# Filter products as two stacked high/low matmuls, sine layers in three pieces, and the sums of squares woven into the first modulation

## The chip, the core and the metric

The kernel runs on one core of one Trainium2 chip. The time is that of one execution on the device, in microseconds (us); lower is better. Engines: TensorE (PE, its weight loads PEld), VectorE (DVE), ScalarE (ACT), GpSimd (POOL) and SyncE (SP), which issues most of the DMAs.

## The reference, cut to what matters

Two layers of a trunk run over 512 latent tokens and 256 context tokens, 1024 channels wide. Each layer has a modulated norm, one input projection into three head groups (Hyena, neighbourhood attention, latent attention), an output projection and an MLP. The change touches three things at the start of the first layer. The modulation:

```python
def _modulation(cond, w_mod, b_mod):
    m = jax.nn.silu(cond) @ w_mod + b_mod
    return jnp.split(m[:, None, :], 6, axis=-1)
```

the norm, which needs the mean square of every token and the first two of the six modulation blocks (shift and scale), and the Hyena filters, which depend on no token at all:

```python
    hdn = jnp.sin(freq[0] * (z @ w1 + b1))
    hdn = jnp.sin(freq[1] * (hdn @ w2 + b2))
    h = (hdn @ w3 + b3).reshape(L, HY_ORDER, 2, HY_DIM)
    ...
    h = h * decay[:, None, None, :]
    return h / (jnp.sum(jnp.abs(h), axis=(0, 2), keepdims=True) + EPS)
```

z has 17 rows, the hidden layers 64 channels, and the last product gives 1024 columns. The filters are made for both layers with the latent length (512) and for the first layer with the context length (256); their spectra are stored in DRAM and read later by the convolution.

## The kernel before, in words

Activations stand transposed: channels on partitions, tokens (NT = 768) along the row. Large products are made in three passes from a high part (rounded to the type fp32r) and a low part (the rest): high by high, high by low, low by high (`gemm`, L262). `split` (L135) makes such a pair with one ScalarE copy and one VectorE subtraction; `wblock` (L253) does so for a block of weights, with three buffers for each of the raw, high and low tiles.

**The order.** The code is a Python program that is unrolled. Generators are woven by hand: `weave` (L791) steps each generator by its rate, and a fill generator by its own. A scheduler then orders each engine's instructions from that program, taking the earliest one that it takes to be ready; on the chip each engine runs its list in order. SP issues the DMAs in its own list, and a load into a buffer still in use holds up everything behind it.

**The start, L1141 to L1193.** `filter_hidden` (L323) loads z, w1, w2 and constants and makes both sine layers of both trunk layers together (64 channels each, 128 partitions). `sin_layer` (L306) takes 768 columns at once: a ScalarE scale and bias from PSUM (L311), five VectorE instructions that bring the argument into range (L313, L314, twice L317, L319), and a ScalarE sine (L321). The second layer's result goes into `h2`, one tile of 65 rows for each trunk layer, row 64 holding ones for the bias. SP then issues the eight blocks of x (L1153), the last filter weights w3 (65 rows), the decay and the first transform matrix, the eight blocks of the modulation's second part (`wm1`, gains), a small matrix, and the eight blocks of its first part (`wm0`, shifts). The 16 modulation blocks (512 KB each) share 13 buffers. `sumsq` (L207) squares a block of x on ScalarE (L213) and adds it on VectorE (L214); the eight blocks are worked between the two sine layers.

`norm_rstd` (L216) sums the squares over channels with TensorE (L221), takes the reciprocal root on VectorE (L122 to L126), and, on its second call, turns it into a row for all partitions (L232, L233). `modulation` (L145) takes two weight blocks a step with TensorE (L150), yields four times, then turns the result (L155, L158) and writes `mods` (L162).

**The filters' fill.** `spectra` (L1166) goes through six filters. For each token tile of a filter `filter_unit` (L340) makes one step: a product of `h2` and w3 (L350, 128x512, plain fp32), a multiplication by the decay (L353), an absolute value (L356, L360) added up (L361), and a sum and a difference (L362 on VectorE, L363 on GpSimd). Its spectrum follows in two or three steps, by turns with the next filter's: the sums (L370), then eight products for each tile of frequencies (L387) with VectorE additions (L391, L395) and a store from GpSimd's queue (L396). There are 20 steps with a product and 16 of spectra. One step runs ahead of the modulations, five beside them (L1184 to L1186); the rest fill the first input products (`mla_in` L633 at half a step for each k, `na_v` L458 at 0.4), and what is left is run after them.

**The norm, L236.** For each of eight channel blocks and both streams: a VectorE multiplication (L241), a ScalarE scale and shift (L242), and the split into high and low (L136, L137). The first input products (L273) need its first block and the first split weights.

## Time and profile before

| | us |
|---|---|
| Runs of the kernel before (three) | 1832.9, 1833.13, 1833.24 |
| Their median | 1833.13 |
| The profiled execution, own time | 1833.48 |
| Its span, first to last instruction | 1831.7 |

The profile is one execution. A line of it gives the source line, engine, operation, output and input by the program's names, shapes and count. PE records: a plain fp32 product leaves two records, a product of fp32r operands one. "Idle before" and the arrow say how long the engine stood still and what ended that. Windows give busy time of each engine with the number of instructions, the granted TensorE clock (1.00 is 2.4 GHz, 0.50 is 1.2 GHz), the share of DMA time and the rate. Matmul ends are modelled, so prices are read from the rhythm of starts where that can be done.

### The profile page before, as it was taken

How to read it: one execution, taken by the hardware profiler on the slowest of the kernel's cores; microseconds unless marked ns; L12 is line 12 of the kernel's file. 1: busy time of each engine (PE TensorE's matmuls, PEld its weight loads, DVE VectorE, ACT ScalarE, POOL GpSimd, SP SyncE). 2: the span in 40 equal slices, each digit the busy share in tenths (PEclk: the TensorE clock that was granted, in tenths of full speed). 3: DMA queues.
4: the chain of work that ended last, by engine and by line, in shares of the span. 5: the costliest groups of instructions: out<-in, count | busy, mean ns of one | idle time of the engine just before them, and what ended most of it. 6: DMA issues, size and time to landing. Idle time of an engine off the chain costs nothing. (4 is left out here: it accounts for less than half of the span.)

```text
span 1831.7 us, 27057 instructions
## 1 busy us (share of the span) xinstructions
PE 1752.5 (96%) x10794; PEld 1499.4 (82%) x10794; DVE 1233.4 (67%) x2247; ACT 754.7 (41%) x1262; POOL 135.8 (7%) x177
## 2 busy tenths in 40 slices
PE   5999977889999999999999999999999999999999
PEld 2788976756788888888888888888777799999997
DVE  5867777787768877767665447787877665555554
ACT  3624326566734412213212224745666653333331
POOL 1134222200000000000000000231200000000000
PEclk8999989989999999999999999999999999999999
DMA  9225423263153333333332222362041022333232
GB/s 344 72 86 167 148 70 108 82 214 113 53 198 115 138 120 134 117 137 115 130 124 60 67 68 95 114 226 81 24 167 41 31 93 94 97 99 93 93 93 81
DMA packets 73389, 206.11 MB, mean 113 GB/s; under 512 B 12556, under 2 KB 24605, under 8 KB 71856
## 3 DMA queue, kind: packets, MB, share of 16 engines
q1 hardware_dynamic: 71664, 199.15, 32.3%
q0 software_dynamic: 1600, 5.24, 0.8%
q8 instruction: 85, 1.39, 0.3%
q14 instruction: 40, 0.33, 0.1%
HBM read 182.35 MB, written 21.23 MB: 111 GB/s over the span
## 5 line engine op out<-in xcount | busy, mean ns | idle before, releaser
L273 PE MATMUL mm<-t,wh 128*128 128x512 f32 (+1 forms) x2496 | 492.5, 317 | 1.9 <-DVE t L1037 1.3
L136 ACT ACTIVATE wh<-wr 128x1024 fp32r<-128x1024 f32 (+2 forms) x176 | 185.2, 1054 | 599.4 <-PE mm L273 541.4
L273 PEld LDWEIGHTS mm<-t,wh 128*128 128x128 f32 x2496 | 371.4, 189 | 37.9 <-issue 1.9
L273 PE MATMUL mm<-t,wl 128*128 128x512 f32 (+1 forms) x1248 | 296.9, 316 | 0.0
L137 DVE TENSOR_TENSOR wl<-wr,wh 128x1024 fp32r<-128x1024 f32 (+2 forms) x176 | 214.1, 1217 | 30.5 <-ACT wh L136 27.1
L273 PE MATMUL mm<-al,wh 128*128 128x512 f32 (+1 forms) x768 | 233.6, 359 | 0.0
L273 PE MATMUL mm<-ah,wl 128*128 128x512 f32 (+1 forms) x768 | 232.2, 356 | 0.0
L1037 DVE SCALAR_TENSOR_TENSOR t<-mm,mods,t 128x512 f32<-128x512 f32 x216 | 136.3, 659 | 140.6 <-PE mm L273 132.7
L273 PE MATMUL mm<-ah,wh 128*128 128x512 f32 (+1 forms) x768 | 230.9, 354 | 0.0
L273 PEld LDWEIGHTS mm<-t,wl 128*128 128x128 f32 x1248 | 193.6, 189 | 16.2 <-DVE wl L137 0.2
L273 PEld LDWEIGHTS mm<-ah,wl 128*128 128x128 f32 x768 | 127.6, 188 | 22.5
L273 PEld LDWEIGHTS mm<-ah,wh 128*128 128x128 f32 x768 | 126.7, 188 | 23.6
L273 PEld LDWEIGHTS mm<-al,wh 128*128 128x128 f32 x768 | 126.3, 188 | 20.1
L191 DVE SCALAR_TENSOR_TENSOR wmp<-wm,t 128x1024 f32<-128x1024 f32 x64 | 78.3, 1224 | 68.3 <-DMA wm<-in_w_modr_dram 68.3
L425 DVE TENSOR_REDUCE mmx<-mm 128x1 f32<-128x768 f32 (+1 forms) x80 | 67.5, 846 | 24.9 <-PE mm L133 24.2
L136 ACT ACTIVATE ah<-relu 128x768 fp32r<-128x768 f32 (+1 forms) x64 | 47.3, 739 | 87.2 <-DVE relu L1100 87.1
L430 ACT ACTIVATE msb<-mm,mmx,qrs 128x768 f32<-128x768 f32 (+1 forms) x80 | 72.2, 904 | 24.8 <-DVE mmx L427 21.1
L1090 DVE TENSOR_SCALAR bb<-mm,cols 128x2 f32<-128x2 f32 x64 | 14.0, 219 | 97.6 <-PE mm L273 97.4
L191 DVE SCALAR_TENSOR_TENSOR wm<-wm,t 128x1024 f32<-128x1024 f32 x64 | 78.1, 1220 | 0.2
L1001 ACT ACTIVATE mpt<-mm 128x768 f32<-128x768 f32 (+1 forms) x80 | 57.6, 725 | 49.9 <-PE mm L1000 49.8
L137 DVE TENSOR_TENSOR al<-relu,ah 128x768 fp32r<-128x768 f32 (+1 forms) x64 | 52.6, 823 | 36.2 <-ACT ah L136 36.1
L1346 PE MATMUL mm<-t,wh 128*128 128x512 f32 x320 | 76.2, 352 | 0.0
(304 smaller groups left out, 2922.0 us busy)
## 6 DMA issues: line engine op xcount, KB each, us to landing
wr<-in_w_ff_dram SPq DMA_DIRECT2D x128, 512.0 KB, 3.6
wm<-in_w_modr_dram SPq DMA_DIRECT2D x64, 512.0 KB, 4.5
wm<-in_w_mod_dram SPq DMA_DIRECT2D x32, 512.0 KB, 8.4
wr<-in_w_in_t_dram SPq DMA_DIRECT2D x18, 512.0 KB, 4.0
qk<-qk_spill SPq DMA_DIRECT2D x9, 576.0 KB, 5.5
qk_spill<-upk SPq DMA_DIRECT2D x12, 384.0 KB, 2.9
kx<-kk POOLq DMA_DIRECT2D x16, 256.0 KB, 2.5
wr<-in_w_in_qk_dram SPq DMA_DIRECT2D x8, 512.0 KB, 4.6
```

Source lines behind the costliest of these rows:

```text
L136: act.activation(hi, src, AF.Copy)
L137: dve.tensor_sub(lo, src, r32(hi))
L191: dve.scalar_tensor_tensor(w if s else junk, w, 1.0, cr[:, s], ALU.mult, ALU.mult, accum_out=mods[:, l, v, k, s:s + 1])
L273: pe.matmul(out_[:, po:po + b - a], wk[wx], mk[mx][:, a:b], start=(k == 0 and i == 0), stop=(k == nk - 1 and i == 2))
L425: dve.tensor_reduce(mx, src, AX.X, ALU.max, negate=True)
L430: act.activation(sb[:, h, :n], src[:, h, :n], AF.Exp, bias=mx[:, h:h + 1], scale=1.0 if scale is None else scale[:, h:h + 1], accum_out=sm ...
L1001: act.activation(pt[:, 0:nkt, qt * 128:(qt + 1) * 128], tt[:, :nkt * 128].rearrange("p (c q) -> p c q", q=128), AF.Copy)
L1037: dve.scalar_tensor_tensor(xT[:, m, a:b], t[:, a:b], mods[:, l, v, m, s:s + 1], xT[:, m, a:b], ALU.mult, ALU.add)
L1090: dve.tensor_scalar(bb, t[:, 768:770], cols[:, l, C_BF1 + f:C_BF1 + f + 1], None, ALU.add)
L1346: pe.matmul(t[:, a:b], ws[wx], half[mx][:, k % 4, a:b], start=(k == ks[0] and i == 0), stop=(k == 7 and i == 2))
```

## The change

- `sin_layer` works on one piece of 256 columns, with three buffers; `filter_hidden` runs three pieces through both layers, the second layer of a piece behind the first layer of the next.
- The last filter product is made from fp32r operands. For each trunk layer there are two tiles of 128 rows for the hidden layer (the high part with the low part stacked under it, or above it for the second trunk layer; and the high part again with rows of ones) and two for w3 (the high part twice; the low part with the bias, also split). Two products of 512 columns replace one.
- `filter_weights` loads w3 raw (64 rows, and the bias row apart) and splits it: three ScalarE copies, two VectorE subtractions, a clear on GpSimd. For the first trunk layer it stands at the start, for the second in the fill.
- SP issues w3, decay and the first transform matrix ahead of x. The modulation blocks share 10 buffers instead of 13.
- The squares are no longer worked between the sine layers but woven with the first modulation (rate 0.6) and the fill (0.5), after two fill steps; then come the sums over channels, and the second modulation with the fill at 0.8.

```diff
--- before.py
+++ after.py
@@ -303,12 +303,10 @@
         sp.dma_start(t, A[name] if src is None else src)
         return t
 
-    def sin_layer(p, outs, zs, hyc, j):
-
-        fb, arg, k = p([128, 1], tag="fb", bufs=2), p([128, NT], tag="arg"), p([128, NT], tag="argk")
-        dve.tensor_mul(fb, hyc[:, j:j + 1], hyc[:, 2 + j:3 + j])
-        for z, a, b in zs:
-            act.activation(arg[:, a:b], z, AF.Identity, bias=fb, scale=hyc[:, j:j + 1])
+    def sin_layer(p, z, fb, hyc, j, n):
+
+        arg, k = p([128, n], tag="arg", bufs=3), p([128, n], tag="argk", bufs=3)
+        act.activation(arg, z, AF.Identity, bias=fb, scale=hyc[:, j:j + 1])
         magic = 12582912.0
         dve.tensor_scalar(k, arg, 1.0 / (2 * math.pi), magic, ALU.mult, ALU.add)
         dve.tensor_scalar(k, k, magic, None, ALU.subtract)
@@ -317,25 +315,56 @@
             dve.scalar_tensor_tensor(arg, k, -c, arg, ALU.mult, ALU.add)
         lim = 3.1415925
         dve.tensor_scalar(arg, arg, -lim, lim, ALU.max, ALU.min)
-        for o, i in outs:
-            act.activation(o, arg[i], AF.Sin)
+        act.activation(arg, arg, AF.Sin)
+        return arg
+
+    def filter_halves(l):
+        return slice(64 * l, 64 * l + 64), slice(64 - 64 * l, 128 - 64 * l), 64 - 64 * l
 
     def filter_hidden(p, h2):
 
         z, w1, w2 = load(p, "hy_z", [17, NT]), load(p, "hy_w1", [17, 128]), load(p, "hy_w2", [128, 128])
-        hyc = load(p, "hy_c", [128, 4])
-        h1 = p([128, NT])
-        for h in h2:
-            pool.memset(h[64:65, :], 1.0)
+        hyc, fb = load(p, "hy_c", [128, 4]), p([128, 2])
+        for l, (_, b) in enumerate(h2):
+            _, other, r = filter_halves(l)
+            pool.memset(r32(b[other]), 0.0)
+            for r_ in (r, r + 32):
+                pool.memset(r32(b[r_:r_ + 1]), 1.0)
         yield
-        for j, (w, src) in enumerate(((w1, z), (w2, h1))):
-            ts = []
-            for a, b in BOTH:
-                ts.append((b_tile()[:, 0:b - a], a, b))
-                pe.matmul(ts[-1][0], w, src[:, a:b], start=True, stop=True)
-            outs = [(h1, slice(0, 128))] if j == 0 else [(h2[0][0:64], slice(0, 64)), (h2[1][0:64], slice(64, 128))]
-            sin_layer(p, outs, ts, hyc, j)
+        dve.tensor_mul(fb, hyc[:, 0:2], hyc[:, 2:4])
+        n = 256
+        s1 = {}
+        for c in range(4):
+            if c < 3:
+                t = b_tile()[:, 0:n]
+                pe.matmul(t, w1, z[:, c * n:(c + 1) * n], start=True, stop=True)
+                s1[c] = sin_layer(p, t, fb[:, 0:1], hyc, 0, n)
+            if c:
+                cs = slice((c - 1) * n, c * n)
+                t = b_tile()[:, 0:n]
+                pe.matmul(t, w2, s1.pop(c - 1), start=True, stop=True)
+                s2 = sin_layer(p, t, fb[:, 1:2], hyc, 1, n)
+                for l, (a, b) in enumerate(h2):
+                    mine, other, _ = filter_halves(l)
+                    act.activation(a[mine, cs], s2[mine], AF.Copy)
+                    dve.tensor_sub(a[other, cs], s2[mine], r32(a[mine, cs]))
+                    act.activation(b[mine, cs], s2[mine], AF.Copy)
             yield
+
+    def filter_weights(l, p):
+
+        raw = p([128, 1024], tag="w3r")
+        hi, lo = p([128, 1024], F32R, tag="w3h"), p([128, 1024], F32R, tag="w3l")
+        mine, other, r = filter_halves(l)
+        sp.dma_start(raw[mine], A["hy_w3"][l, 0:64])
+        sp.dma_start(raw[r:r + 1], A["hy_w3"][l, 64:65])
+        pool.memset(r32(lo[other]), 0.0)
+        for x in (mine, other):
+            act.activation(hi[x], raw[mine], AF.Copy)
+        dve.tensor_sub(lo[mine], raw[mine], r32(hi[mine]))
+        act.activation(lo[r:r + 1], raw[r:r + 1], AF.Copy)
+        dve.tensor_sub(lo[r + 32:r + 33], raw[r:r + 1], r32(lo[r:r + 1]))
+        return hi, lo
 
     def filter_unit(l, st, o, h2, fc, dec, w3, p):
 
@@ -347,8 +376,9 @@
         def time_domain():
             for tt in range(ntt):
                 ph = b_tile()
-                pe.matmul(ph, h2[:, (t0 + tt) * 128:(t0 + tt + 1) * 128], w3[:, o * 512:(o + 1) * 512],
-                          start=True, stop=True)
+                for i in range(2):
+                    pe.matmul(ph, h2[i][:, (t0 + tt) * 128:(t0 + tt + 1) * 128], w3[i][:, o * 512:(o + 1) * 512],
+                              start=(i == 0), stop=(i == 1))
                 h = p([128, 2, 256], tag="h", bufs=2)
                 dve.tensor_mul(h, ph.rearrange("p (d c) -> p d c", d=2),
                                dec[:, t0 + tt, :].unsqueeze(1).to_broadcast([128, 2, 256]))
@@ -1141,7 +1171,7 @@
     na, vp = NA(), Pool("nav0", "right")
     na.v, na.rs, kr = vp([128, 6, 256]), vp([128, 6, 4]), vp([128, 6, 32])
     fp = Pool("filters", "right")
-    h2 = [fp([65, NT]) for _ in range(DEPTH)]
+    h2 = [(fp([128, NT], F32R), fp([128, NT], F32R)) for _ in range(DEPTH)]
     wmp = Pool("wm_start")
     xp = Pool("x0", "right")
     xT, acc = xp([128, KD, NT]), xp([128, NT])
@@ -1149,25 +1179,28 @@
     psum_banks(0)
     hidden = filter_hidden(hid, h2)
     next(hidden)
+    w3s = filter_weights(0, fp)
+    dec = load(fp, "hy_decay", [128, 6, 256])
+    fcs = [load(fp, "dft_fx", [128, 2, 4, 256])]
     for k in range(KD):
         sp.dma_start(xT[:, k], A["xT"][:, k])
-    w3s = load(fp, None, [65, 1024], A["hy_w3"][0], "w3")
-    dec = load(fp, "hy_decay", [128, 6, 256])
-    fcs = [load(fp, "dft_fx", [128, 2, 4, 256])]
-    wm1 = [mod_weights(0, 1, k, wmp, 13) for k in range(KD)]
+    wm1 = [mod_weights(0, 1, k, wmp, 10) for k in range(KD)]
     fcs.append(load(fp, "dft_fc", [128, 1, 4, 128]))
-    wm0 = [mod_weights(0, 0, k, wmp, 13) for k in range(KD)]
-    for k in range(KD):
-        if k % 4 == 0:
-            next(hidden)
-        sumsq(acc, xT, k, NT, xp)
+    wm0 = [mod_weights(0, 0, k, wmp, 10) for k in range(KD)]
+    for _ in hidden:
+        pass
     hid.close()
+
+    def squares_in():
+        for k in range(KD):
+            sumsq(acc, xT, k, NT, xp)
+            yield
 
     def spectra():
         w3, before = w3s, iter(())
         for l, st, o in ((0, 0, 0), (0, 0, 1), (0, 1, 0), (0, 1, 1), (1, 0, 0), (1, 0, 1)):
             if (l, st, o) == (1, 0, 0):
-                w3 = load(fp, None, [65, 1024], A["hy_w3"][l], "w3")
+                w3 = filter_weights(l, fp)
             t, f = filter_unit(l, st, o, h2[l], fcs[st], dec, w3, fp)
             for _ in t:
                 yield
@@ -1182,8 +1215,10 @@
     rstd = norm_rstd(acc, NT, sc)
     fill = spectra()
     next(fill)
+    next(fill)
+    weave((squares_in(), 1.0), (modulation(0, 1, wmp, ws=wm1), 0.6), fill=(fill, 0.5))
     next(rstd)
-    weave((chain(modulation(0, 1, wmp, ws=wm1), modulation(0, 0, wmp, ws=wm0)), 1.0), fill=(fill, 0.5))
+    weave((modulation(0, 0, wmp, ws=wm0), 1.0), fill=(fill, 0.8))
     rb = next(rstd)
     wmp.close()
     hp_ = Pool("h0")
```

## Rows read from the trace of the kernel before

**Rows 1.** The page: busy time and share of the span of each engine
```profile
PE 1752.5 (96%) x10794; PEld 1499.4 (82%) x10794; DVE 1233.4 (67%) x2247; ACT 754.7 (41%) x1262; POOL 135.8 (7%) x177
```

**Rows 2.** Windows; columns: length, PE, PEld, DVE, ACT, POOL, clock, DMA, GB/s
```profile
5.00:44.00 39.00, 22.82 (x140) 11.08 (x144) 23.62 (x47) 14.94 (x21) 3.95 (x4) 0.87 1.02 387
10.00:48.50 38.50, 23.29 (x173) 12.13 (x172) 25.58 (x52) 15.62 (x25) 4.92 (x5) 0.87 0.93 353
26.00:34.00 8.00, 7.75 (x46) 4.67 (x46) 3.51 (x14) 1.62 (x3) 0.89 (x1) 0.50 1.03 411
...
53.40:150.00 96.60, 96.09 (x536) 81.24 (x535) 62.98 (x123) 36.95 (x73) 25.32 (x33) 1.00 0.23 81
```

**Rows 3.** SP's timeline from 0 to 100 us; columns: start, length, engine
```profile
10.93 10.81 SPq L142 DMA_DIRECT2D wm<-in_w_mod_dram  x8
...
23.97 9.78 SPq L142 DMA_DIRECT2D wm<-in_w_mod_dram  x8
```

**Rows 4.** TensorE's timeline at the start; columns as in rows 3
```profile
26.25 2.04 PE L350 MATMUL b<-w,t 65*128 65x512 f32 x2 [5.40 <-issue]
28.09 2.56 PE L221 MATMUL b<-ones,t 128*128 128x1 f32 x12
30.58 3.64 PE L150 MATMUL b<-wm,cst 128*32 128x256 f32 x32
...
42.06 3.23 PE L150 MATMUL b<-wm,cst 128*32 128x256 f32 x56
...
50.57 3.16 PE L387 MATMUL b<-sd,t 128*128 128x256 f32 x10
53.38 0.93 PE L273 MATMUL mm<-t,wh 128*128 128x512 f32 x3
```

**Rows 5.** VectorE's timeline, 44 to 64 us
```profile
46.33 0.24 DVE L162 TENSOR_TENSOR mods<-b,cols 128x8 f32<-128x8 f32 x2 [1.70 <-PE b L158]
...
47.45 1.22 DVE L137 TENSOR_TENSOR wl<-wr,wh 128x1024 fp32r<-128x1024 f32 x1
48.59 2.90 DVE L241 TENSOR_TENSOR t<-t,rb 128x512 f32<-128x512 f32 x6
...
60.77 1.23 DVE L137 TENSOR_TENSOR wl<-wr,wh 128x1024 fp32r<-128x1024 f32 x1
```

**Rows 6.** TensorE's groups by form, 53.4 to 150 us; columns: count, busy us, mean ns
```profile
L350 PE MATMUL b<-w,t 65*128 65x512 f32 x28 | 14.3, 592 | 0.0
```

**Rows 7.** TensorE's timeline, 66 to 77 us
```profile
66.54 3.69 PE L387 MATMUL b<-sd,t 128*128 128x256 f32 x16
69.88 1.06 PE L273 MATMUL mm<-t,wh 128*128 128x512 f32 x4
...
72.34 0.52 PE L273 MATMUL mm<-t,wl 128*128 128x512 f32 x2
...
73.39 0.51 PE L273 MATMUL mm<-t,wl 128*128 128x512 f32 x2
73.74 1.02 PE L350 MATMUL b<-w,t 65*128 65x512 f32 x2
...
75.30 0.51 PE L273 MATMUL mm<-t,wl 128*128 128x512 f32 x2
```

**Rows 8.** VectorE's groups by form, 5 to 64 us; columns as in rows 6
```profile
L353 DVE TENSOR_TENSOR h<-b,t 128x512 f32<-128x512 f32 x6 | 4.1, 690 | 6.3 <-PE b L350 6.3
L317 DVE SCALAR_TENSOR_TENSOR arg<-argk,arg 128x768 f32<-128x768 f32 x4 | 3.8, 955 | 0.1
...
L362 DVE TENSOR_TENSOR sd<-h 128x256 f32<-128x256 f32 x5 | 2.7, 531 | 0.1
L137 DVE TENSOR_TENSOR t<-t,t 128x256 fp32r<-128x256 f32 x6 | 2.6, 426 | 0.0
L137 DVE TENSOR_TENSOR wl<-wr,wh 128x1024 fp32r<-128x1024 f32 x2 | 2.4, 1224 | 0.0
...
L313 DVE TENSOR_SCALAR argk<-arg 128x768 f32<-128x768 f32 x2 | 1.1, 560 | 3.7 <-ACT arg L311 3.7
```

## Prediction

> **What bounds the kernel now.** I read the page first. TensorE is busy for 96% of the span [rows 1], so over most of the kernel whatever TensorE no longer has to do is gained, and whatever other engines do beside it costs nothing. The exception is the start, where the whole change lies; so I then took windows over the first 150 us [rows 2]. They split it in two. From 53.4 to 150 us TensorE is busy 96.09 of 96.60 us while VectorE is busy 62.98: **here TensorE is the bound**, and the reader should see that the filter steps which are woven into the input products each take their place in its queue. Before that the 16 DMA engines are full from 5 to 44 us, with TensorE busy 22.8 of 39 us and VectorE 23.6. The loads of the first two modulation blocks are issued one after another from 10.9 to 33.8 us [rows 3]. VectorE's timeline shows how this start ends: the second modulation's values are written at 46.33, the first multiplication of the norm stands at 48.59, and TensorE's first input product at 53.38 [rows 4, 5]. The norm gives VectorE and ScalarE no pause afterwards. So the start ends with the last modulation weights, and two sums decide about this change: what leaves TensorE's queue after 53.4 us, and by how much the norm starts later or earlier than 48.59.
>
> **What TensorE gets rid of.** There are 20 filter products, each 128x512 with plain f32 operands, two records apiece. 28 of the 40 records, so 14 products, run after 53.4 us [rows 6]. Their price is read from the rhythm of the queue: a round of six input products (2304 columns) comes back after 1.05 us (72.34 to 73.39), and with one filter product in it after 1.91 us (73.39 to 75.30) [rows 7]. One costs 0.86 us. The stacked form is two products of the same rounded type as the input products, 512 columns each: 2 x 512/2304 x 1.05 = 0.47 us. Contraction over 128 rows instead of 65 has no row of its own; I bound the pair between 0.47 and the old 0.86 and take 0.47, because the input products it is priced by contract over 128 rows.
>
> The new weave takes eleven filter steps before the norm where the old one takes six. Counting the yields: two steps ahead, five beside the first modulation (ten rounds at 0.5), four beside the second (0.8). That is eight products, the sums, and both spectra of the first filter. Before, six products and ten of the 32 spectrum records ran ahead of 53.38. So 12 products are left for the bound part, not 14, and 22 spectrum records leave it: 16 take from 66.54 to 69.88, 0.209 us each [rows 7]. The sum: 14 x 0.86 - 12 x 0.47 + 22 x 0.209 = 12.0 - 5.6 + 4.6 = **11.0 us less on TensorE**.
>
> **What the start pays on VectorE.** Each row is for one instruction [rows 8].
> - Sine layers: ten instructions of 768 columns (six at 0.56, four at 0.955: 7.2 us) become 30 of 256. The two-operand form has a row at 256 columns, 0.426. The one-operand form has none; it lies between 0.19 (a third of 0.56) and 0.43, and 0.56 with the fixed part of about 0.16 that the two-operand rows show (0.955 for 768, 0.426 for 256) gives 0.30. So 18 x 0.30 + 12 x 0.43 = 10.5, that is 3.3 more.
> - Splitting the hidden layer: six subtractions of 256 columns, 2.6.
> - Splitting the last weights: one subtraction of 64x1024 and one of a single row of 1024. The first is 1.22 as the 128-row form; the second lies between 0.2 and 1.22, and I take 1.22, since the rows go by columns. 2.4.
> - Five more filter steps: three products at 0.69 + 0.69 + 0.53 and two spectra at 0.43 + 2 x 0.69, the row of the same shape: 9.3.
>
> Together 17.6 us. From 10 to 48.5 us VectorE is idle for 38.5 - 25.6 = 12.9 us [rows 2]. The sums of squares only move within the start. So 4.7 us do not fit. Not all of the idle time can be used, but the last product and the last spectrum (3.7 us) need not stand ahead of the norm either. I take **5 us later** for the norm, between 0 and 8.
>
> A rule of the Trainium skill speaks against the pieces: "VectorE: DVE Perf Modes", section on the TRN2 errata, says that a fixed latency is paid by every instruction, so that many small tiles pay it many times, and advises 512 elements or more. Its table (58 cycles and one per element, half for the one-operand form) would make the layers 1.1 us dearer instead of 3.3 and the whole some 2 us better, about 1825; the trace has 0.955 where the table gives 0.86, so the measurement decides, and the section itself says the table runs low.
>
> **What lies beside other work.** ScalarE gets 12 copies, shorter sines and three copies of 1024 columns in the start; the pieces let it run while VectorE works on the next one, and its own load, 15.6 us before against VectorE's 25.6 [rows 2], stays below VectorE's. The clears go to GpSimd, busy for 4.9 of 38.5 us [rows 2]. The second layer's weight split (two VectorE and three ScalarE instructions) comes after 100 us, where VectorE has a third of its time free [rows 2]; TensorE has input products to do meanwhile. If that cover went, it would cost about 5 us once.
>
> On SP's queue the filter weights, the decay and the first transform matrix now pass the eight loads of x, so x lands later; nothing needs it before the squares, which are later too. The bytes ahead of the modulation weights stay the same. With 10 buffers instead of 13, six loads of the second block wait for a product of the first instead of three. The old rate would issue the third load at about 26.4 us (23.97 + 2 x 1.22) [rows 3]; the first modulation product ran at 30.58, behind the filters' hidden layer and the squares' sum [rows 4]. Now that sum stands behind it, so it can start when its weights land. If it did not, the hole would be 4.6 us and hidden in the 5 us above; the input weights behind these loads in SP's queue would wait too.
>
> **The sum.** -11.0 + 5 = -6.0 against the profiled execution: 1833.48 - 6.0 = 1827.5. The median of the runs is 0.35 lower, so **1827.1**. Its own range is 1823 to 1831 (norm 1 to 8 us late). About 0.2%, 3.7 us, is what a measurement of this kernel can tell from no change.
>
> **The rivals.**
> - *The weights' low half behind the norm: about 1834, no change.* The first input products need a VectorE subtraction (1.22) that before slipped in at 47.45, just ahead of the norm; the next block's came at 60.77, 12.2 us after the norm's start [rows 5]. With VectorE full until the norm, the first block's can land there too: the products then really run from 48.6 + 5 + 12.2 + 1.2 = 67, not 58.4. TensorE can do eight high products (1.4 us) ahead; 7.2 us are lost and the gain is spent. For it: the idle time is used up. Against it: VectorE may pause while the second modulation is awaited.
> - *TensorE's queue becomes the start's chain: about 1838, slower.* The sum of squares now needs VectorE to have done 10 + 2.4 + 13.1 + five products (9) + 6.7 = 41 us. If the second modulation stands behind it in TensorE's order, we have 41 + 2.6 for the row sums + 3.7 for its 64 records (56 took 3.23) [rows 4], and both spectra are woven between: 32 records, at half clock 0.42 each, 13.4 us. Products and transposes bring the values to about 62.5 instead of 46.33, 16 us late: -11 + 16 = +5. It decides once they are written after 57.3. For it: the granted clock was 0.50, the 1.2 GHz level, from 26 to 34 us, after TensorE had been idle for 5.4 us [rows 2, 4]. Against it: the modulation's products are free to go ahead when the sum is not ready, and the second spectrum can fall behind them. "TensorE: Matmul & The Clock Gate", Part 1, in the Trainium skill has the same: throttled is the default and activity releases it; the trace agrees, 0.50 there and 1.00 from 53.4 us.
> - *More of the gain stays: about 1822.* The norm passes the late filter steps and starts on time: -11.
> - *The stacked pair costs what the f32 product costs: about 1832, no change.* Both have two records. Then 12 x 0.39 = 4.7 us are missing. The rhythm of the input products speaks against it.
>
> **How the numbers follow.** Forecast 0.52, of which 0.06 are within 0.2%; low half 0.18, of which 0.02 fall on the slower side; stacked pair not cheaper 0.04; slower chain 0.16; more of the gain 0.10. Faster 0.46 + 0.10 = 0.56; same 0.06 + 0.16 + 0.04 = 0.26; slower 0.16 + 0.02 = 0.18. The range takes in the slower chain's price and most of the best case: 1821 to 1838.
>
> **What would show it.** Filter products after the start should come back in a round of about 1.5 us instead of 1.9. The norm's first multiplication should stand at 52 to 56 us and VectorE be busy over 90% from 10 us until then. If the first input product stands more than 6 us behind the norm's first multiplication, or only high products stand there, it is the low half. If the values of the second modulation are written after 57 us, it is the queue. I would be wrong in kind if TensorE showed idle time after 70 us that it did not have, or if VectorE showed long pauses in the start.

## The result, and the profile after

| | us |
|---|---|
| Runs of the changed kernel (four) | 1841.93, 1842.96, 1844.3, 1844.49 |
| Their median | 1843.63 |
| Runs of the kernel before beside them | 1832.51 to 1833.24, median 1833.02 |
| Ratio, 95% interval | 1.0057, 1.0041 to 1.0073 |
| The profiled execution, own time and span | 1844.49, 1842.7 |

The change made the kernel some 10.5 us slower; 1827.1 was predicted. In the experiments below the kernel before itself took 1831.5 to 1843.9 us from one execution to the next, so they are told as ratios to it.

TensorE's timeline of the changed kernel shows where it happens, in the start. L400 are the filter's sums (L370 before), L380 the stacked pair (L350), L417 the spectra (L387). It answers to [rows 4].

```profile
28.22 1.07 PE L150 MATMUL b<-wm,cst 128*32 128x256 f32 x16
41.62 1.87 PE L400 MATMUL b<-ones,facc 128*128 128x1 f32 x8 [12.33 <-DVE facc L391]
43.41 2.79 PE L150 MATMUL b<-wm,cst 128*32 128x256 f32 x24
...
48.04 1.40 PE L221 MATMUL b<-ones,t 128*128 128x1 f32 x12
49.37 0.64 PE L150 MATMUL b<-wm,cst 128*32 128x256 f32 x8
...
50.20 1.03 PE L417 MATMUL b<-sd,t 128*128 128x256 f32 x4
51.16 0.64 PE L150 MATMUL b<-wm,cst 128*32 128x256 f32 x8
51.73 1.56 PE L417 MATMUL b<-sd,t 128*128 128x256 f32 x6
...
62.27 0.64 PE L150 MATMUL b<-wm,cst 128*32 128x256 f32 x8
...
67.53 1.02 PE L400 MATMUL b<-ones,facc 128*128 128x1 f32 x8 [2.09 <-DVE facc L391]
...
70.23 2.99 PE L273 MATMUL mm<-t,wh 128*128 128x512 f32 x7 [0.69 <-ACT t L136]
121.19 0.39 PE L380 MATMUL b<-w3h,t 128*128 128x512 f32 x1
121.42 0.39 PE L380 MATMUL b<-w3l,t 128*128 128x512 f32 x1
121.65 0.29 PE L131 MATMUL b<-wh,t 128*128 128x288 f32 x1
```

Three things are to be seen. The first filter's sums stand ahead of the last 24 records of the first modulation and hold them for 12.33 us, until VectorE has added up the absolute values. Between the products of the second modulation (49.37 to 62.91) stand 32 spectrum records. And the first input product comes at 70.23 instead of 53.38. The pair itself takes 0.46 us (121.19 to 121.65). VectorE's timeline gives the other side, and answers to [rows 5]:

```profile
30.96 6.28 DVE L214 TENSOR_TENSOR t<-t,sq 128x768 f32<-128x768 f32 x6
37.16 0.68 DVE L383 TENSOR_TENSOR h<-b,t 128x512 f32<-128x512 f32 x1
...
40.89 0.68 DVE L391 TENSOR_TENSOR facc<-facc,habs 128x512 f32<-128x512 f32 x1
...
63.88 0.24 DVE L162 TENSOR_TENSOR mods<-b,cols 128x8 f32<-128x8 f32 x2 [0.17 <-PE b L158]
...
65.03 1.22 DVE L137 TENSOR_TENSOR wl<-wr,wh 128x1024 fp32r<-128x1024 f32 x1
...
67.64 3.49 DVE L241 TENSOR_TENSOR t<-t,rb 128x512 f32<-128x512 f32 x7
```

From 26 to 41.6 us VectorE works almost without a break (14.91 of 15.60 us): the last pieces and splits, then the squares, and only then the last steps of the first filter, whose sum TensorE waits for. The second modulation's values are written at 63.88 instead of 46.33, the norm starts at 67.64 instead of 48.59, with the first input weights split (65.03) ahead of it. The windows of the changed kernel (columns as in [rows 2]) show what follows:

```profile
10.00:40.00 30.00, 11.53 (x58) 5.26 (x58) 25.97 (x52) 19.96 (x37) 4.05 (x4) 0.91 0.96 385
40.00:60.00 20.00, 17.88 (x126) 11.28 (x127) 10.05 (x32) 3.20 (x7) 3.53 (x6) 0.80 0.43 145
68.00:72.00 4.00, 3.31 (x12) 2.20 (x13) 4.00 (x10) 3.71 (x8) 0.00 (x0) 0.56 0.20 74
72.00:76.00 4.00, 4.00 (x15) 3.43 (x16) 4.00 (x10) 4.00 (x9) 0.00 (x0) 0.58 0.00 0
76.00:80.00 4.00, 2.92 (x15) 1.86 (x14) 4.00 (x10) 4.00 (x9) 0.00 (x0) 1.00 0.00 0
```

From 40 to 60 us VectorE is busy only half the time: now it waits for TensorE. The granted clock, 1.00 at 60 us, is 0.56 and 0.58 from 68 to 76, behind the two pauses of TensorE at 65.4 and 69.5 (2.09 and 0.69 us), and the input products begin near the lower level (0.50).

Later, first instructions of a line in both traces give the distance. At the start of the convolution's input (151.06 before, 158.86 after) it is 7.8 us: of the 16.85 us, 9.05 have come back. At 283.1 it is 7.4, at the end 11.0. The last 3.6 us build up where nothing of the change runs, and most of them are the granted clock. Around 350 us and around 1160 us TensorE waits 2.9 us in both traces; behind that the clock differs. From 1164 to 1180 us it is 0.52, 0.50, 0.50 and 0.77 (windows of 4 us), in the kernel before, from 1156 to 1172, 0.77, 0.50, 0.88 and 1.00, and over this place the distance grows from 8.7 to 11.4 us. The run with the pieces alone (below), which has the old order, loses 2.7 us there in the same way (0.51, 0.50, 0.50, 0.78). Why the lower level lasts longer in one execution than in another no run here shows.

### The profile page after: what moved, and what is told of

Same layout as the page of the kernel before. It is cut to its first block, busy times and chain, and to the rows that moved or that the text cites. A ratio compares the mean times of both kernels' runs of the same rounds, so it can differ in the third digit from the quotient of the medians.

```text
span 1842.7 us, 27128 instructions
## 1 busy us (share of the span) xinstructions
PE 1753.8 (95%) x10798; PEld 1503.0 (82%) x10798; DVE 1242.0 (67%) x2276; ACT 765.3 (42%) x1285; POOL 139.3 (8%) x183
## 5 line engine op out<-in xcount | busy, mean ns | idle before, releaser
L273 PEld LDWEIGHTS mm<-ah,wl 128*128 128x128 f32 x768 | 127.6, 188 | 22.4
L136 ACT ACTIVATE ah<-relu 128x768 fp32r<-128x768 f32 (+1 forms) x64 | 47.3, 739 | 86.9 <-DVE relu L1130 86.7
```

The source lines that it names most:

```text
L136: act.activation(hi, src, AF.Copy)
L273: pe.matmul(out_[:, po:po + b - a], wk[wx], mk[mx][:, a:b], start=(k == 0 and i == 0), stop=(k == nk - 1 and i == 2))
```

## The experiments

Ratios to the kernel before are compared here, and not times; where a us stands beside a ratio, it is the ratio times 1833.1. A ratio of 1.001 is 1.8 us. The change itself was not run again beside them; its row has the four runs above.

| Run | ratio, 95% interval | first input product, us | second modulation's values, us |
|---|---|---|---|
| the kernel before | 1 | 53.4 | 46.3 |
| the change | 1.0057 (1.0041, 1.0073) | 70.2 | 63.9 |
| fill 0.4 and 0.8 | 1.0022 (1.0006, 1.0038) | 68.5 | 61.2 |
| fill 0.5 and 0.2 | 1.0025 (1.0010, 1.0040) | 62.2 | 54.2 |
| fill 0.4 and 0.2 | 1.0007 (0.9994, 1.0020) | 60.6 | 54.0 |
| fill 0.1 and 0.2 | 1.0032 (1.0019, 1.0046) | 54.6 | 47.9 |
| fill 0.1 and 0.5 | 0.9989 (0.9972, 1.0005) | 53.8 | 48.7 |
| change with the f32 product | 1.0094 (1.0072, 1.0116) | 71.5 | 65.5 |
| change, splits on GpSimd | 1.0061 (1.0041, 1.0081) | 71.6 | 65.3 |
| old order, pieces and pairs | 0.9982 (0.9969, 0.9995) | 52.4 | 46.4 |
| before with the pairs alone | 0.9992 (0.9980, 1.0003) | 54.6 | 49.2 |
| before with the pieces alone | 0.9992 (0.9976, 1.0008) | 52.0 | 47.1 |
| old order, sums later from the 2nd filter | 0.9989 (0.9976, 1.0002) | 51.9 | 46.8 |
| the same, splits on GpSimd | 1.0000 (0.9986, 1.0013) | 53.4 | 47.3 |
| old order, sums later from the 3rd filter | 0.9968 (0.9954, 0.9981) | 52.1 | 46.9 |

### The sums behind the first modulation

```diff
-    weave((squares_in(), 1.0), (modulation(0, 1, wmp, ws=wm1), 0.6), fill=(fill, 0.5))
+    weave((squares_in(), 1.0), (modulation(0, 1, wmp, ws=wm1), 0.6), fill=(fill, 0.4))
```

> The changed kernel with the fill beside the first modulation at 0.4 instead of 0.5, so that the first filter's sums stand behind all eight blocks of the first modulation in TensorE's list; the spectra still stand between the second modulation's products. Theory (order of TensorE's list): the wait of 12.3 us before the first filter's sums goes, the second modulation's loads have no hole, the norm starts 8 to 12 us earlier than 67.6 us and the time is 1832 to 1837 us. Rival 1 (VectorE has too much to do before the norm): VectorE's work is the same, so the time stays within 3 us of 1843.6. Rival 2 (ten buffers leave the hole in the loads): the hole stays, the time stays above 1838.

Ratio 1.0022, that is 1837. The expected step failed: the norm came only 1.7 us earlier. The wait before the sums went, and the next instruction took it over: the transposes of the first modulation's row (L158) waited 9.09 us for ScalarE's copy of that row.

```profile
43.69 0.69 PE L158 MATMUL b<-ident,wr 128*128 128x128 f32 x2 [9.09 <-ACT wr L155]
```

The run was better later, with a granted clock of 0.79 from 68 to 76 us (0.57 in the change).

### The spectra behind the second modulation

```diff
-    weave((modulation(0, 0, wmp, ws=wm0), 1.0), fill=(fill, 0.8))
+    weave((modulation(0, 0, wmp, ws=wm0), 1.0), fill=(fill, 0.2))
```

> The changed kernel with the fill beside the second modulation at 0.2 instead of 0.8: no spectrum record stands between the second modulation's products, but the first filter's sums still stand ahead of the last three blocks of the first. Theory (order of TensorE's list): the wait of some 12 us before the sums stays, the second modulation's values are written 6 to 10 us earlier than 63.9 us, some 24 spectrum records (0.209 us each, 5 us) go into the stretch where TensorE is the bound, so 1838 to 1842 us. Rival 1 (VectorE): two or three fill steps fewer ahead of the norm are worth 3 to 5 us of VectorE, given back later on TensorE: 1842 to 1845. Rival 2 (ten buffers): the hole stays, 1840 to 1844.

Ratio 1.0025, 1837.7, just below the theory's range. Its 64 products of the second modulation ran from 49.51 to 53.17 in one go, and the first input product came 8 us earlier, though the sums still waited (10.63 us). So of the 17 us, some 8 to 10 are the spectra between the products.

### Both

```diff
-    weave((squares_in(), 1.0), (modulation(0, 1, wmp, ws=wm1), 0.6), fill=(fill, 0.5))
+    weave((squares_in(), 1.0), (modulation(0, 1, wmp, ws=wm1), 0.6), fill=(fill, 0.4))
...
-    weave((modulation(0, 0, wmp, ws=wm0), 1.0), fill=(fill, 0.8))
+    weave((modulation(0, 0, wmp, ws=wm0), 1.0), fill=(fill, 0.2))
```

> Both of these together (fill rates 0.4 and 0.2). Theory (order of TensorE's list): neither the sums nor the spectra stand ahead of a modulation product, the norm starts at 49 to 55 us, and the time is 1827 to 1834 us (14 stacked pairs 0.40 us cheaper each are left after the start, against ten spectrum records that no longer run ahead of it and a norm up to 5 us late). Rival 1 (VectorE): the norm comes 4 us earlier at most, 1839 to 1844. Rival 2 (ten buffers): above 1836.

Ratio 1.0007, 1834.4: the time is the theory's at its upper edge, the norm is not (57.92). ScalarE's timeline of this run shows why:

```profile
35.97 0.84 ACT L213 ACTIVATE sq<-t 128x768 f32<-128x768 f32 x1 [0.22 <-DVE t L214]
38.69 0.63 ACT L390 ACTIVATE habs<-h 128x512 f32<-128x512 f32 x1 [1.88 <-DVE h L383]
40.35 0.63 ACT L390 ACTIVATE habs<-h 128x512 f32<-128x512 f32 x1 [1.03 <-DVE facc L391]
41.82 0.63 ACT L386 ACTIVATE facc<-h 128x512 f32<-128x512 f32 x1 [0.84 <-DVE h L383]
42.35 0.36 ACT L155 ACTIVATE wr<-b 128x256 f32<-128x256 f32 x1
```

The modulation's products had ended by 34 us, but its row (L155) stands behind the filter's absolute values in ScalarE's list, and those wait for VectorE. The second modulation's loads had no hole in this run (SP issued them from 22.8 to 33.2 us, against 22.4 to 44.9 in the change), with the same ten buffers: the hole was a consequence, and the buffers are not the cause.

### Nearly no fill beside the modulations

```diff
-    weave((squares_in(), 1.0), (modulation(0, 1, wmp, ws=wm1), 0.6), fill=(fill, 0.5))
+    weave((squares_in(), 1.0), (modulation(0, 1, wmp, ws=wm1), 0.6), fill=(fill, 0.1))
...
-    weave((modulation(0, 0, wmp, ws=wm0), 1.0), fill=(fill, 0.8))
+    weave((modulation(0, 0, wmp, ws=wm0), 1.0), fill=(fill, 0.2))
```

> The changed kernel with nearly no filter steps beside the modulations (rates 0.1 and 0.2 instead of 0.5 and 0.8); stacked product, pieces, squares by turns with the first modulation, ten buffers and the order of the loads stay. What it tells apart: in the run with rates 0.4 and 0.2 the row of the first modulation on ScalarE still stood behind the filter's absolute values, which waited for VectorE until 42.35 us. Theory (in-order lists of TensorE and ScalarE: work that needs VectorE's filter steps stands ahead of the modulations): the first modulation ends at 34 to 38 us, the values of the second are written at 46 to 50 us, first input product at 52 to 56 us, time 1828 to 1834 us. Rival 1 (pieces and splits on VectorE are dear in themselves): first input product at 58 us or later, 1834 to 1839 us. Rival 2 (ten buffers): a hole in the loads, 1834 us or more.

The start came out as the theory said (values at 47.85, first input product at 54.59), the time did not: 1.0032, 1839, as dear as the first rival said, without the late start by which that rival was to be known. A start in time is not enough. TensorE's wait before the sums, and the windows of this run:

```profile
51.86 1.87 PE L400 MATMUL b<-ones,facc 128*128 128x1 f32 x8 [2.00 <-DVE facc L391]
```

```profile
52.00:56.00 4.00, 4.00 (x15) 3.46 (x15) 4.00 (x9) 4.00 (x8) 0.00 (x0) 0.50 0.39 112
56.00:60.00 4.00, 4.00 (x17) 3.27 (x16) 4.00 (x10) 4.00 (x9) 0.00 (x0) 0.67 0.00 0
60.00:68.00 8.00, 6.27 (x33) 4.95 (x33) 8.00 (x17) 8.00 (x17) 0.00 (x0) 1.00 0.22 56
```

TensorE had waited 2.00 us for the sums until 51.86; behind that the granted clock was 0.50, the 1.2 GHz level, and the input products began at half speed.

### The first spectrum as cover

```diff
-    weave((squares_in(), 1.0), (modulation(0, 1, wmp, ws=wm1), 0.6), fill=(fill, 0.5))
+    weave((squares_in(), 1.0), (modulation(0, 1, wmp, ws=wm1), 0.6), fill=(fill, 0.1))
...
-    weave((modulation(0, 0, wmp, ws=wm0), 1.0), fill=(fill, 0.8))
+    weave((modulation(0, 0, wmp, ws=wm0), 1.0), fill=(fill, 0.5))
```

> The changed kernel with the fill rates 0.1 and 0.5 (0.5 and 0.8 in it, 0.1 and 0.2 in the run with the fill behind): the first modulation is free of filter steps, but the first filter's sums and twelve records of its spectrum stand between the second modulation and the first input product, as in the kernel before. Theory (what the run with the fill behind lost after a start in time, it lost because TensorE stood still before its first input products, worked at a granted clock of 0.50 to 0.67 from 52 to 60 us, and had all 32 spectrum records still to do): first input product at 51 to 55 us, granted clock over 0.9 from 52 to 60 us, time 1828 to 1833 us. Rival (the new weave costs some 6 us by itself, by VectorE's pieces and splits or by the ten buffers, wherever the fill stands): 1836 us or more, as with the fill behind.

Ratio 0.9989, no worse than the kernel before: pieces, pairs, ten buffers, the squares by turns and the order of the loads are all still in it, and only two rates of the change are altered. The loss is the fill's place. Its windows, for the same stretches:

```profile
52.00:56.00 4.00, 3.94 (x20) 2.88 (x18) 3.94 (x9) 4.00 (x10) 0.00 (x0) 1.00 0.39 112
56.00:60.00 4.00, 3.86 (x19) 2.84 (x19) 4.00 (x9) 4.00 (x9) 0.00 (x0) 1.00 0.01 4
```

Against the run before it 0.0043, 7.9 us, are won; the two intervals leave anything from 4 to 12. In the two profiled executions it is 3.3 us, and these are there by 81 us. Twelve spectrum records at 0.209 us done ahead of the input products are 2.5 of it. What the clock adds was not separated: in these 8 us it is worth 3.3 at most (4 x 0.50 + 4 x 0.33), and in the run before it TensorE waits for VectorE again at 61.85 and 64.26 us (0.74 and 0.98), so that part of it would have been waited out at the upper level too.

### The f32 product in the new order

```diff
-                for i in range(2):
-                    pe.matmul(ph, h2[i][...], w3[i][...], start=(i == 0), stop=(i == 1))
+                pe.matmul(ph, h2[...], w3[...], start=True, stop=True)
...
```

> The changed kernel with the plain f32 last product (no splits of the hidden layer and of the weights, 65 rows); the new order, pieces and ten buffers stay. Theory (order): the first filter's sums still stand ahead of the last three blocks of the first modulation and the spectra between the products of the second, so the norm is some 14 to 19 us late, the filter products after the start cost 0.86 us instead of 0.46 (10 of them, 4 us): 1841 to 1848 us. Rival 1 (VectorE's 5 us of splits are the cause): 1836 to 1840 us. Rival 3 (the stacked product itself costs time later): below 1836 us.

Ratio 1.0094, 1850, beyond the theory's range and far from both rivals. The sums came earlier, at 38.84 after a wait of 4.79 us, since VectorE has no splits, and yet the second modulation began at 48.67 and the first input product at 71.5: with the spectra in its list TensorE is not done sooner. What makes this run slower than the change is one more wait, in TensorE's and VectorE's timelines:

```profile
71.53 3.55 PE L273 MATMUL mm<-t,wh 128*128 128x512 f32 x8
81.46 1.01 PE L273 MATMUL mm<-t,wl 128*128 128x512 f32 x2 [6.38 <-DVE wl L137]
```

```profile
80.19 1.21 DVE L137 TENSOR_TENSOR wl<-wr,wh 128x1024 fp32r<-128x1024 f32 x1
```

Eight high products run, and then TensorE stands for 6.38 us until the low half of the first weights is there. Its split stands 13.7 us behind the norm's first multiplication (66.49) in this run's list of VectorE, and ahead of it in the change's. So the difference of the two ratios, some 7 us, is not what the pairs are worth in this order: in the profile the run is 8.0 us behind the change by 81 us, of which 6.4 are this wait and 1.3 the later first input product, and 10.9 by 159 us. The 2.9 between are what is left for ten products at 0.86 instead of 0.46, 4 us.

### The splits on GpSimd, in the new order

```diff
-                    dve.tensor_sub(a[other, cs], s2[mine], r32(a[mine, cs]))
+                    pool.tensor_sub(a[other, cs], s2[mine], r32(a[mine, cs]))
...
-        dve.tensor_sub(lo[mine], raw[mine], r32(hi[mine]))
+        pool.tensor_sub(lo[mine], raw[mine], r32(hi[mine]))
...
-        dve.tensor_sub(lo[r + 32:r + 33], raw[r:r + 1], r32(lo[r:r + 1]))
+        pool.tensor_sub(lo[r + 32:r + 33], raw[r:r + 1], r32(lo[r:r + 1]))
```

> The changed kernel with the splits of the hidden layer and of the last weights on GpSimd instead of VectorE (5 us of VectorE in the start, 2.4 us later); rates and lists stay. It asks whether the amount of VectorE's work counts in the new order. If VectorE's queue ahead of the first filter's sums is what TensorE waits for, the sums come 3 to 5 us earlier than 41.6 us and the time is 1838 to 1842 us. If only the order counts, whatever VectorE has to do, the time stays at 1842 to 1845 us. If GpSimd's slower subtractions (1.0 us for 128x256) come ahead of the first products, it is later: over 1846 us.

Ratio 1.0061, the change's own; the sums came at 43.49 instead of 41.62. The run does not answer its question, because VectorE was not relieved: it stood while GpSimd worked (2.43 us for an instruction of 0.29, last section).

### The old order with pairs and pieces

```diff
+    for k in range(KD):
+        sp.dma_start(xT[:, k], A["xT"][:, k])
...
-    for _ in hidden:
-        pass
+    for k in range(KD):
+        if k % 2 == 0:
+            next(hidden)
+        sumsq(acc, xT, k, NT, xp)
...
-    next(fill)
-    weave((squares_in(), 1.0), (modulation(0, 1, wmp, ws=wm1), 0.6), fill=(fill, 0.5))
     next(rstd)
-    weave((modulation(0, 0, wmp, ws=wm0), 1.0), fill=(fill, 0.8))
+    weave((chain(modulation(0, 1, wmp, ws=wm1), modulation(0, 0, wmp, ws=wm0)), 1.0), fill=(fill, 0.5))
```

> The changed kernel with the stacked product, the pieces and the ten buffers, but the order of the kernel before: x loaded first, two squares after each step of the hidden layers, both modulations in one chain with the fill at 0.5, one fill step ahead. Theory (order of TensorE's list): the norm starts within 5 us of 48.6, the 14 pairs after it keep 5.6 us, so 1826 to 1832 us, faster than the kernel before. Rival 1 (VectorE's extra instructions cost more than they bring, whatever the order): 1836 to 1844. Rival 2 (ten buffers leave a hole of 7 us in the loads): 1834 to 1838.

Ratio 0.9982, 1829.8: the theory's range, and neither rival. But the expected 5.6 us of the pairs are not there. In its profiled execution the first input product is 1.0 us earlier than before and the last 1.3 us. Two places show where they went; TensorE's and VectorE's timelines of this run:

```profile
58.59 0.72 PE L273 MATMUL mm<-t,wh 128*128 128x512 f32 x2 [0.31 <-DVE t L137]
...
60.47 0.72 PE L273 MATMUL mm<-t,wh 128*128 128x512 f32 x2 [0.17 <-DVE t L137]
...
121.19 1.02 PE L400 MATMUL b<-ones,facc 128*128 128x1 f32 x8 [1.53 <-DVE facc L391]
```

```profile
57.85 1.02 DVE L137 TENSOR_TENSOR t<-t,t 128x512 fp32r<-128x512 f32 x2
...
59.73 1.02 DVE L137 TENSOR_TENSOR t<-t,t 128x512 fp32r<-128x512 f32 x2
...
61.00 1.22 DVE L137 TENSOR_TENSOR wl<-wr,wh 128x1024 fp32r<-128x1024 f32 x1
```

From 58 to 63 us the input products follow the norm's pace, 1.88 us a block; the second split of weights stands at 61.00 here and at 60.77 before [rows 5], so what TensorE has won by then, it waits out. And at 121 us the sums of a filter wait for VectorE, with a granted clock of 0.93 from 124 to 140 us (1.00 in the kernel before). From 53.4 to 150 us TensorE is idle for 3.4 us (0.5 before), and the clock costs some 1.7 (8 x 0.08 from 116 us, 8 x 0.13 from 124 us); from the first input product to 151 us 0.6 are won. That is 5.2 of the 5.6.

### Pairs alone, pieces alone

The kernel before with the pairs (whole sine layers), and with the pieces (f32 product), each as in the change:

```diff
-                pe.matmul(ph, h2[:, ...], w3[:, ...], start=True, stop=True)
+                for i in range(2):
+                    pe.matmul(ph, h2[i][:, ...], w3[i][:, ...], start=(i == 0), stop=(i == 1))
...
-    w3s = load(fp, None, [65, 1024], A["hy_w3"][0], "w3")
+    w3s = filter_weights(0, fp)
```

> The kernel before (whole sine layers, squares between the layers, x first, both modulations in one chain with the fill at 0.5) with the stacked product alone, its splits in it, and ten buffers. Theory: 14 pairs after the start save 0.40 us each, 5.6 us, of which new waits for VectorE give some back, as in the run with the old order and pieces (1.4 us in its profile, 3.3 us by its ratio): 1827 to 1831 us. Rival 1 (the pieces cost some 3 us of VectorE in the start): 1825 to 1828 us, some 3 us better than that run. If the split of the hidden layer and of the weights is what delays the start, 1833 us or more.

```diff
-    def sin_layer(p, outs, zs, hyc, j):
+    def sin_layer(p, z, fb, hyc, j, n):
...
-        if k % 4 == 0:
+        if k % 2 == 0:
             next(hidden)
```

> The kernel before with the sine layers in three pieces alone (plain f32 last product, old order, 13 buffers). Theory: the start hangs on the last modulation weights, the 3.3 us more of VectorE lie beside the loads: 1831 to 1835 us, no difference. Rival 1 (VectorE's work before the norm is the cause): 1836 to 1838 us.

The second of these ran with ten buffers, not with the 13 that its expectation names.

Both 0.9992, 1831.6: just above the theory's range for the pairs and above its first rival's, within the theory's range for the pieces. The pairs alone are not 3 us better than with the pieces but, if anything, 2 us worse: the pieces are not what costs, and their 3.3 us of VectorE lie beside the loads (first input product at 52.0, earlier than before). Neither alone is told from no change.

### The sums one step later

```diff
-            for _ in t:
+            for i, _ in enumerate(t):
                 yield
-                for _ in before:
+                for _ in before if i or n < 2 else ():
                     yield
                     break
```

> The run with the old order (stacked product, pieces) and the sums of each filter but the first one step later in the fill. That run lost at 121 us: TensorE waited 1.5 us for the sums of a filter, and the granted clock was 0.92 and 0.87 in the 16 us behind. Theory (of the 5.6 us that the pairs save, new waits and the clock behind them take 3 to 4): the wait goes, 2 to 3 us better than that run, 1827 to 1830 us, ratio 0.996 to 0.998. Rival (the pairs do not save that much after the start): no difference to that run, ratio 0.998 to 0.999.

> The run before it (old order, pieces, sums one step later) with the splits of the hidden layer and of the second layer's last weights on GpSimd (2.6 us less on VectorE in the start, 2.4 us less after 100 us). Theory: VectorE is not what sets the start in the old order, so the start stays; the filter steps after 100 us wait less: 0 to 2 us better than the run before it, 1826 to 1829 us. Rival (GpSimd's subtractions are slow and late): 1 to 3 us worse.

0.9989 and 1.0000: the rivals' numbers. In the first run the wait at 121 us was gone, but another loss had come: moved sums now stood next to the input products' own (TensorE's timeline of the first of the two runs, and its windows, TensorE alone).

```profile
78.26 0.95 PE L400 MATMUL b<-ones,facc 128*128 128x1 f32 x8
79.23 1.50 PE L681 MATMUL b<-ones,csq 128*128 128x1 f32 x12
...
81.69 2.12 PE L681 MATMUL b<-ones,csq 128*128 128x1 f32 x12
```

```profile
82.00:84.00 2.00, 2.00 (x12) 0.59 0.13 49
84.00:86.00 2.00, 2.00 (x7) 0.50 0.00 0
86.00:88.00 2.00, 2.00 (x8) 0.50 0.40 84
```

The clock is the lower of the two levels here; the loss of these 6 us is some 2.8 (2 x 0.41 + 4 x 0.50). GpSimd's splits in the second run cost some 1.4 us, as its rival had it: the intervals of the two ratios overlap, but the medians of the twelve executions of each, taken by turns, are 1834.61 and 1835.98.

### The sums later from the third filter on

```diff
-                for _ in before if i or n < 2 else ():
+                for _ in before if i or n < 3 else ():
```

> The run with the old order (stacked product, pieces) with the sums one step later from the third filter's spectrum on (in the run with the sums later it was from the second on, which put the sums of the second filter next to the sums of the input products at 78 us, after which the granted clock was 0.50 to 0.59 from 82 to 88 us). Theory (what the pairs save is lost again to new waits of 1.5 us for the sums at 121 us and to the clock behind them): the start and the stretch to 100 us stay as in the run with the old order, the wait at 121 us goes, 2 to 3.5 us better than it: ratio 0.9955 to 0.9975. Rival (VectorE paces this stretch, and a wait taken away comes back elsewhere): no better than that run, ratio 0.998 to 1.000.

Ratio 0.9968 (0.9954 to 0.9981), 5.9 us faster than the kernel before: the theory's number. With the run with the old order it is one of two versions whose interval lies below 1, so faster than both kernels; the intervals of these two overlap (0.9954 to 0.9981 and 0.9969 to 0.9995), and that it is the faster of them rests on the trace. TensorE's timeline and windows of this run:

```profile
121.92 0.95 PE L400 MATMUL b<-ones,facc 128*128 128x1 f32 x8
```

```profile
108.00:124.00 16.00, 16.00 (x104) 14.81 (x103) 13.49 (x27) 6.23 (x16) 7.20 (x10) 1.00 0.18 67
124.00:140.00 16.00, 16.00 (x97) 14.81 (x96) 9.70 (x21) 3.63 (x7) 3.96 (x6) 1.00 0.30 111
```

No wait is left before the sums, TensorE is busy for all 32 us at 1.00, and by the first L526 of the old numbering (283.1 before) it is 3.7 us ahead; the run with the old order was 1.4 ahead there. Its profiled execution, 1830.96, is 2.5 us below that of the kernel before; by the ratio it is more. So a good part of the pairs' 5.6 us can be kept (2.5 by the profile, all by the ratio), once no sum stands where VectorE is late.

## Why the prediction was wrong

**The step that failed is "5 us later for the norm, between 0 and 8".** The norm started 19 us later (67.64 against 48.59), the first input product 16.85. The step summed VectorE's work and charged what did not fit into its idle time. VectorE was not full: 10.05 of 20 us from 40 to 60. What cost was that instructions which need VectorE's filter steps stand in the lists of TensorE and ScalarE ahead of the modulations.

**The mechanism was the second rival,** "TensorE's queue becomes the start's chain", at 0.16: the second modulation stood in TensorE's list behind a sum that waits for VectorE, with the spectra between its products. The sum was another one. The rival has the sum of squares hold the queue; it was the first filter's, and the squares' sum (48.04) came behind it without a wait of its own. That the values came at 63.88 where it has about 62.5 is in part luck. VectorE's 41 us fit (41.62), but from there to the second modulation it was 7.75 us and not 2.6, since three blocks of the first modulation were still to do, and that modulation with its 32 spectrum records took 13.54 and not 17.1, since the clock was not at half all the time (0.80 from 40 to 60 us). Its price, +5 in the sum, is half of the 11.0 in the profile. What I held against it was wrong: the modulation's products were not free to go ahead, since each engine's list is fixed, and the second spectrum did not fall behind them. It lacked the clock of 0.56 under the first input products, whose cost was not separated (TensorE waits for VectorE again at 77.75 us, 0.61), and the 3.6 us after 283 us. The first rival, the weights' low half behind the norm, at 0.18, was not what happened in the change (split at 65.03, norm at 67.64), but it came in the run with the f32 product: 6.38 us where 7.2 were priced.

**"11.0 us less on TensorE".** The prices were right: 0.46 us for a pair (0.47 taken), and a round of input products with a pair comes back after 1.51 us (94.44 to 95.95), as the prediction expected. The count was not: ten pairs and not eight stood ahead of the first input product, so ten were left and the term is 12.0 (12.0 - 4.6 + 4.6). Of these 9.05 came back by 158.86. That the stretch from 53.4 us on is TensorE's alone was not: with the old order, where only the pairs' 5.6 us were at stake, 1.3 showed in the profile and 3.3 by the ratio. The norm paces the products until 63 us, and a filter's sums wait as soon as TensorE is ahead.

**The costs on VectorE.** Pieces and splits cost what was summed (the one-operand piece 0.29 us where 0.30 was taken, the single row 1.22 as taken) and delayed nothing in the old order. The 1.1 us by which the layers would be dearer by the table are 1.2 when the sum is done again, which changes nothing. The doubt about the holes in the loads, priced at 4.6 us and hidden, was right in place (no load from 40 to 44 us), but the hole was a consequence of the held queue and not a cause.

**The tell-tales.** The norm's first multiplication was past 56, VectorE was not over 90% busy until then, the second modulation's values were written after 57: the queue, as the prediction had set it down. VectorE also showed the long pauses in the start (3.29 us before 47.43, 2.83 before 56.23) by which the prediction was to be wrong in kind.

## What to carry to other kernels

When work is woven ahead of a critical chain, don't only ask whether an engine has room: go through the fixed list of each engine and find the instructions that stand ahead of the chain and wait for a third engine. Weaving less was better here, but not least: with twelve independent spectrum records just ahead of the first input products TensorE did not stand still there, the granted clock was 1.00 instead of 0.50, and the run was faster. After every edit the lists have to be gone through again: with the f32 product one split of weights had moved behind the norm, and that alone cost 6.38 us. A saving on a busy engine shows only where no other engine follows closely behind; look for the waits of a few tenths that are already there.

## What the runs showed of the hardware

VectorE stood while GpSimd worked. In the run with the splits on GpSimd, GpSimd's and VectorE's timelines:

```profile
12.22 2.64 POOL L364 TENSOR_TENSOR w3l<-w3r,w3h 64x1024 fp32r<-64x1024 f32 x1 [5.21 <-ACT w3h L363]
17.99 2.65 POOL L366 TENSOR_TENSOR w3l<-w3r,w3l 1x1024 fp32r<-1x1024 f32 x1 [3.12 <-ACT w3l L365]
```

```profile
12.25 2.90 DVE L315 SCALAR_TENSOR_TENSOR arg<-argk,arg 128x256 f32<-128x256 f32 x2
...
18.36 2.43 DVE L317 TENSOR_SCALAR arg<-arg 128x256 f32<-128x256 f32 x1
```

The 0.29 us instruction at L317 took 2.43 us and ended at 20.79, just behind GpSimd's (20.64); the two at L315, 0.75 together at 17.69, took 2.90 and ended at 15.15, GpSimd's at 14.86. The Trainium skill, "SBUF — State Buffer", section "SBUF: two separate sides", has a port pair that the two engines share, and that one of them holds for its whole instruction while the other is blocked; the trace agrees, VectorE's instructions ending 0.15 and 0.29 us behind GpSimd's.

In the run with the sums later the granted clock fell to 0.59 and 0.50 behind 82 us, though TensorE had been busy for 3.86 of the 4 us before (windows of 78 to 80 and 80 to 82); what it did there was mostly one-column sums. In the run with the sums later from the third filter on, where they stand apart, it stayed at 1.00 from 76 to 92. That the sums are the cause was not tested by itself. The same wait can be followed by a short or a long stretch at the lower level: the 2.9 us near 1160 us by some 7 us in the kernel before and by some 14 in the change. And a subtraction of one row of 1024 took 1.22 us on VectorE, the same as 64 rows (1.21).
